# Merging two softmax maps: from VectorE and GpSimd arithmetic to a ScalarE scaling and an accumulating DMA

## The chip, the cores and the metric

The kernel runs on one core of a Trainium2 chip. A core has TensorE (PE in the profile, its weight loads PEld), VectorE (DVE), ScalarE (ACT), GpSimd (POOL), and SyncE (SP), from whose queue this kernel issues its DMAs. The metric is the time of one execution in microseconds on the device, the median of several runs.

## The reference

The program is one layer of a diffusion backbone: 2048 latent tokens and 128 context tokens of width 1024, with a differential attention (4 heads, two softmax maps each) beside a gated short convolution, an output projection and a SwiGLU feed-forward. All is float32. The change concerns the attention, where latent queries attend to 2048 latent and 128 cached keys:

```python
s = jnp.einsum('bqhmd,bkhmd->bhmqk', qblk.astype(jnp.float32), kf) * ATTN_SCALE
p = jax.nn.softmax(s, axis=-1)
a = p[:, :, 0] - lam * p[:, :, 1]          # the two maps of a head, merged
return jnp.einsum('bhqk,bkhe->bqhe', a, vf)
```

Each head's output is then RMS-normalised, which makes it insensitive to a common factor of a row. The kernel uses that: it merges the unnormalised exponentials as e0 + wt * e1, where wt is -lam times the ratio of the two row sums.

## The kernel before

Every float32 matmul is made of products of a high and a low part (`split`, L79: ScalarE casts to the high part, L81, another engine subtracts for the low one, L82). The work goes through these stages: modulation and input projection (to about 384 us), attention with the convolution as filler (384 to about 1316 us), output projection, and the feed-forward.

The attention loops over 4 heads and, within a head, over 8 groups of 256 latent queries and one group of 128 context queries (`work`, L790). For each group `softmaxes` (L485) is called, and after it `values` (L523) for the group before, so that the scores of one group stand in the program ahead of the values of the last.

`softmaxes` goes over the query tiles of 128 of its group, two for a latent group, so there are 64 latent tiles. For each of the two maps of a tile it takes a buffer e of 128 x 2176 float32 and fills it in five chunks of 436 or 432 keys: TensorE makes the scores (L499, into one of three PSUM banks), VectorE scales them into e and takes their maximum (L502). One ScalarE exponential over the 2176 columns, with the row sum, follows (L507). When both maps are there, VectorE works out wt (L510 to L513), and the maps are merged into e[0]: GpSimd scales the last 960 columns of e[1] by wt (L516) and adds them to those of e[0] (L517), and VectorE does the first 1216 columns in one operation (L518).

`values` transposes the merged tiles block by block (17 blocks of 128 keys, two to a PSUM bank, both query tiles, L543), splits them (L546) and multiplies them by the values (L534 to L536). Behind it, the head norm runs with small steps on GpSimd (L90, L91, L573).

There are five buffers for e and, while the convolution lasts, a sixth that every sixth request takes (`e_tile`, L478). e[1] is free after the merge; e[0] after the last transpose of its group.

The convolution is the filler: a generator that yields after some TensorE work (L605 to L667), and `pump` (L778) takes from it at a rate set by `RATE`, after each score chunk and each pair of transposed blocks. Its inputs fu come by 256 KB DMAs from SyncE's queue (L597), five buffers for each part; its tail is a row of GpSimd steps (L657 to L661).

The code is written with a framework that plans the order of each engine's instructions when the program is built, by program order as priority and a simulated timeline, and places the semaphores. Each engine then runs its list in that order.

Of the kernel before, what the change touches and what calls it, by code (L numbers as in the profile page):

```python
# [11 lines left out]
AF = mybir.ActivationFunctionType  # L12
ALU = mybir.AluOpType
# [16 lines left out]
LI = 0.2  # L30

KC = ((0, 436), (436, 436), (872, 436), (1308, 436), (1744, 432))

POOLW = 960
WLV = (2,)
RAWS = 6
RATE = (670, 1500)
# [3 lines left out]
def layer(ctx, tc, x_prompt, x_sample, cache_k, cache_v, cond, w_ada, b_ada, gcol,  # L41
# [3 lines left out]
    V, S, G, T = nc.vector, nc.scalar, nc.gpsimd, nc.tensor  # L45
# [432 lines left out]
    def e_tile():  # L478

        ecount[0] += 1  # L480
        if x_fu is not None and ecount[0] % 6 == 0:
            return pf.tile([P, NALL], F32, tag="e", name="e")
        return pa.tile([P, NALL], F32, tag="e", name="e", bufs=5)

    def softmaxes(qt, nq, km, kcs):  # L485

        nk = sum(n for _, n in kcs)
        sm = pa.tile([P, 2, 2], F32, tag="sm", name="sm", bufs=3)
        r = pa.tile([P, 2, 2], F32, tag="r", name="r", bufs=3)
        out = []  # L490
        for t in range(nq):
            e = []
            for m in range(2):
                et = e_tile()
                mx = pa.tile([P, 5], F32, tag="mx", name="mx", bufs=4)
                for ci, (k0, n) in enumerate(kcs):
                    ps = pss.tile([P, 512], F32, tag="s", name="s")
                    for s in range(2):
                        mm = T.matmul(ps[:, :n], qt[:, s, m, t * P:(t + 1) * P], km[m][:, k0:k0 + n],  # L499
                                      start=(s == 0), stop=(s == 1))  # L500
                        marks.append(mm.ins)
                    V.tensor_scalar(et[:, k0:k0 + n], ps[:, :n], SCALE, None, op0=ALU.mult, op1=ALU.max,  # L502
                                    accum_out=mx[:, ci:ci + 1])
                    pump()
                nm = pa.tile([P, 1], F32, tag="nm", name="nm", bufs=4)
                V.tensor_reduce(nm, mx[:, :len(kcs)], axis=AX.X, op=ALU.max, negate=True)  # L506
                S.activation(et[:, :nk], et[:, :nk], AF.Exp, bias=nm, scale=1.0, accum_out=sm[:, t, m:m + 1])  # L507
                e.append(et)

            V.reciprocal(r[:, t, :], sm[:, t, :])  # L510
            wt = pa.tile([P, 1], F32, tag="wt", name="wt", bufs=3)
            V.tensor_scalar(wt, r[:, t, 1:2], neglam, sm[:, t, 0:1], op0=ALU.mult, op1=ALU.mult)
            V.tensor_scalar(wt, wt, 1e30, -1e30, op0=ALU.min, op1=ALU.max)  # L513
            cut = nk - (POOLW if nk > 128 else 0)
            if cut < nk:
                G.tensor_scalar(e[1][:, cut:nk], e[1][:, cut:nk], wt, 1.0, op0=ALU.mult, op1=ALU.mult)  # L516
                G.tensor_tensor(e[0][:, cut:nk], e[0][:, cut:nk], e[1][:, cut:nk], op=ALU.add)  # L517
            V.scalar_tensor_tensor(e[0][:, :cut], e[1][:, :cut], wt, e[0][:, :cut],  # L518
                                   op0=ALU.mult, op1=ALU.add)
            out.append(e[0])  # L520
        return out, r

# [255 lines left out]
    def pump():  # L778

        nonlocal credit  # L780
        credit += RATE[x_fu is None]
        while credit > 0:
            with tc.issue_after(marks[-1]) if marks else ExitStack():
                c = next(todo)
            if not c:
                credit = 0.0
                break
            credit -= c
# [5 lines left out]
    for n, (h, i) in enumerate(work):  # L794
        if i == 0:
            qt = hb.pop("q") if n == 0 else load_q(h, 0, 256)
            km, kp = hb.pop("k") if n == 0 else load_keys(h)
            vts = load_values(h)
        lat = i < 8
        if i > 0:  # L800
            qt = load_q(h, i, 256 if lat else 128)
        if lat:
            ar = softmaxes(qt, 2, km, KC)
        else:
            ar = softmaxes(qt, 1, [kp[:, 0, :], kp[:, 1, :]], ((0, 128),))
        if pending:
            values(*pending)
        pending = (h, i, ar, vts if lat else vts[17:], 17 if lat else 1)
        ready = max(0, n - 28)
# [347 lines left out]
```

## Time and profile before

| | us |
|---|---|
| median of 3 runs | 3038.56 (3036.72 to 3039.07) |
| the profiled execution | 3041.68 |
| its span, first to last instruction | 3039.9 |
| attention stage (384 to 1316 us) | 932 |
| TensorE busy in that stage | 893.3 |
| VectorE, ScalarE, GpSimd busy there | 738.1, 553.1, 467.0 |
| granted TensorE clock, whole span | 0.987 |

A line of the profile's groups reads: line of the kernel, engine, operation, what is written <- what is read, shape, number; then busy time and mean ns of one; then the idle time of the engine just before, and what ended it. In the views of time a row begins with its start and its length in us. In the digits, each is the busy share of a fortieth of the span in tenths. A wait is put down to the semaphore that came last.

### The profile page before, as it was taken

To read this page: it belongs to the slowest core of one execution; us is meant where nothing else is said; L and a number is where in the kernel's file an instruction comes from. 1 tells how busy PE (TensorE), PEld (TensorE's weight loads), DVE (VectorE), ACT (ScalarE), POOL (GpSimd) and SP (SyncE) were. 2 spreads that over 40 slices of the span, in tenths; PEclk is the share of its full clock that TensorE was granted. 3 is DMA by queue.
4 is the path that set the end of the run, shared out by engine and by line. 5 is a ranking of instruction groups with operands and counts; after the bars stand their busy time and mean duration, and the time that the engine had idled before them with its cause. 6 is when DMAs were issued, how large, how long until landed. Compare 5 with 4: busy or idle time off the path is not lost.

```text
span 3039.9 us, 47168 instructions
## 1 busy us (share of the span) xinstructions
PE 2902.1 (95%) x16925; PEld 2647.5 (87%) x16925; DVE 1961.1 (65%) x3768; ACT 1466.6 (48%) x2707; POOL 1204.6 (40%) x1106
## 2 busy tenths in 40 slices
PE   6999989999999999999999999999999999999998
PEld 4777789998999998988889989999999998788886
DVE  5998477877888888753367765566555554554443
ACT  5333346665556655554455554445444443434332
POOL 5332135455455454522255654555444440111110
PEclk9999999999999999999999999999999999999999
DMA  8886654454354454457554565445633335766663
GB/s 320 286 306 232 197 177 134 133 168 137 119 178 125 120 165 117 127 182 220 173 159 146 151 196 197 152 152 178 231 102 100 104 103 199 243 218 221 217 218 119
DMA packets 353483, 533.64 MB, mean 176 GB/s; under 512 B 33344, under 2 KB 264928, under 8 KB 351456
## 3 DMA queue, kind: packets, MB, share of 16 engines
q1 hardware_dynamic: 353248, 530.62, 54.2%
q8 instruction: 133, 2.18, 0.3%
q14 instruction: 102, 0.84, 0.1%
HBM read 402.18 MB, written 128.34 MB: 175 GB/s over the span
## 4 chain that ended last, share of the span: by engine, by line
PE 63%; DVE 12%; DMA 10%; issue 8%; POOL 4%; ACT 3%; SPq 0%; DVEq 0%; POOLq 0%; ACTq 0%
PE s L499 7%; PE psg L956 6%; PE psg L954 6%; PE psg L955 6%; PE psy L1086 5%; PE psy L1085 5%; PE psy L1084 5%; PE t L543 3%; DMA u2d<-hl 3%; DVE jv L137 2%; DVE wi L82 2%; PE psx L722 2%; PE psx L723 2%; PE psx L721 2%; PE o L536 2%
## 5 line engine op out<-in xcount | busy, mean ns | idle before, releaser
L954 PE MATMUL psg<-u,wi 128*128 128x384 f32 (+1 forms) x1848 | 607.2, 332 | 26.0 <-ACT wi L81 10.3
L956 PE MATMUL psg<-u,wi 128*128 128x384 f32 (+1 forms) x1848 | 597.1, 329 | 10.0 <-DVE wi L82 10.0
L955 PE MATMUL psg<-u,wi 128*128 128x384 f32 (+1 forms) x1848 | 606.5, 328 | 0.0
L502 DVE TENSOR_SCALAR_CACHE_REDUCE e<-s 128x436 f32<-128x436 f32 (+2 forms) x648 | 373.8, 600 | 85.6 <-PE s L499 68.4
L954 PEld LDWEIGHTS psg<-u,wi 128*128 128x128 f32 x1848 | 349.3, 189 | 36.9 <-ACT wi L81 14.2
L956 PEld LDWEIGHTS psg<-u,wi 128*128 128x128 f32 x1848 | 347.8, 189 | 14.0 <-DVE wi L82 13.7
L499 PE MATMUL s<-km,qt 128*128 128x436 f32 (+1 forms) x1280 | 345.7, 374 | 12.3 <-DVE e L502 8.3
L955 PEld LDWEIGHTS psg<-u,wi 128*128 128x128 f32 x1848 | 350.1, 189 | 0.3
L82 DVE TENSOR_TENSOR wi<-st,wi 128x512 fp32r<-128x512 f32 x264 | 245.2, 932 | 157.7 <-ACT wi L81 154.8
L82 DVE TENSOR_TENSOR wo<-rawo,wo 128x1024 fp32r<-128x1024 f32 x132 | 167.0, 1265 | 252.8 <-ACT wo L81 252.8
L507 ACT ACTIVATE e<-e,nm 128x2176 f32<-128x2176 f32 (+1 forms) x136 | 274.0, 2014 | 78.5 <-DVE nm L506 77.8
L81 ACT CAST wi<-st 128x512 fp32r<-128x512 f32 x264 | 163.2, 619 | 279.2 <-PE psg L956 191.1
L1086 PE MATMUL psy<-wo,hhl 128*128 128x512 f32 x748 | 286.1, 391 | 1.8 <-DVE hhl L82 1.8
L1085 PE MATMUL psy<-wo,hhl 128*128 128x512 f32 x748 | 286.7, 391 | 0.9 <-DVE wo L82 0.9
L1084 PE MATMUL psy<-wo,hhl 128*128 128x512 f32 x748 | 286.3, 391 | 0.0
L81 ACT CAST wo<-rawo 128x1024 fp32r<-128x1024 f32 x132 | 139.1, 1054 | 295.4 <-PE psy L1086 285.2
L82 DVE TENSOR_TENSOR wi<-raw,wi 128x512 fp32r<-128x512 f32 x198 | 233.2, 1194 | 35.6 <-ACT wi L81 29.3
L499 PEld LDWEIGHTS s<-km,qt 128*128 128x128 f32 x1280 | 210.6, 192 | 23.3 <-DVE e L502 14.1
L81 ACT CAST ath<-t 128x512 fp32r<-128x512 f32 (+2 forms) x292 | 157.4, 554 | 114.8 <-PE t L543 112.2
L82 DVE TENSOR_TENSOR atl<-t,ath 128x512 fp32r<-128x512 f32 (+2 forms) x292 | 187.2, 649 | 36.4 <-ACT ath L81 35.6
L1057 POOL TENSOR_TENSOR rr<-rr,mhalf 128x1 f32<-128x1 f32 x17 | 13.1, 779 | 452.7 <-DVE rr L1056 452.7
L916 POOL TENSOR_TENSOR st<-raw,st 128x512 f32<-128x512 f32 x66 | 87.2, 1321 | 252.4 <-DVE wi L82 252.4
(261 smaller groups left out, 6991.5 us busy)
## 6 DMA issues: line engine op xcount, KB each, us to landing
raw<-in_w_fi SPq DMA_DIRECT2D x132, 512.0 KB, 4.2
rawo<-in_w_fo SPq DMA_DIRECT2D x132, 512.0 KB, 3.5
fu<-ud SPq DMA_DIRECT2D x256, 256.0 KB, 4.5
raw<-in_w_ada SPq DMA_DIRECT2D x64, 512.0 KB, 5.9
u2d<-hl SPq DMA_DIRECT2D x42, 512.0 KB, 3.9
u<-u2d SPq DMA_DIRECT2D x14, 1536.0 KB, 10.1
hr<-hid SPq DMA_DIRECT2D x110, 192.0 KB, 3.5
hid<-hid SPq DMA_DIRECT2D x88, 192.0 KB, 3.6
```

The costliest lines, as they stand in the source:

```text
L81: S.copy(h, src)
L82: (eng or V).tensor_tensor(l, src, h.bitcast(F32), op=ALU.subtract)
L499: mm = T.matmul(ps[:, :n], qt[:, s, m, t * P:(t + 1) * P], km[m][:, k0:k0 + n], start=(s == 0), stop=(s == 1))
L502: V.tensor_scalar(et[:, k0:k0 + n], ps[:, :n], SCALE, None, op0=ALU.mult, op1=ALU.max, accum_out=mx[:, ci:ci + 1])
L507: S.activation(et[:, :nk], et[:, :nk], AF.Exp, bias=nm, scale=1.0, accum_out=sm[:, t, m:m + 1])
L543: T.transpose(tp[:, j, t * P:(t + 1) * P], a[t][:, (k0 + j) * P:(k0 + j + 1) * P], ident)
L954: T.matmul(ps, h[:, ks], u[:, 0, kt, :n], start=start and kt == 0, stop=False, skip_group_check=not start)
L955: T.matmul(ps, h[:, ks], u[:, 1, kt, :n], start=False, stop=False, skip_group_check=not start)
L956: T.matmul(ps, l[:, ks], u[:, 0, kt, :n], start=False, stop=kt == 3, skip_group_check=not start)
L1084: T.matmul(banks[i][:, b, :], hh, woh_[:, bs], start=(f == 0), stop=False)
L1085: T.matmul(banks[i][:, b, :], hh, wol_[:, bs], start=False, stop=False)
L1086: T.matmul(banks[i][:, b, :], hl, woh_[:, bs], start=False, stop=(f == NF - 1))
```

## The change

For the latent tiles the merge is done in two pieces, columns 0 to 1151 and 1152 to 2175. For each piece ScalarE multiplies e[1] by wt in place (a Copy activation with wt as the scale), and a DMA issued from GpSimd's queue adds the piece to e[0] in place. The context tiles (128 columns) keep VectorE's single operation. The GpSimd arithmetic of L516 and L517 and the constant that set its share are gone.

```diff
-POOLW = 960
...
             V.tensor_scalar(wt, wt, 1e30, -1e30, op0=ALU.min, op1=ALU.max)
-            cut = nk - (POOLW if nk > 128 else 0)
-            if cut < nk:
-                G.tensor_scalar(e[1][:, cut:nk], e[1][:, cut:nk], wt, 1.0, op0=ALU.mult, op1=ALU.mult)
-                G.tensor_tensor(e[0][:, cut:nk], e[0][:, cut:nk], e[1][:, cut:nk], op=ALU.add)
-            V.scalar_tensor_tensor(e[0][:, :cut], e[1][:, :cut], wt, e[0][:, :cut],
-                                   op0=ALU.mult, op1=ALU.add)
+            if nk > 128:
+                for ks in (slice(0, 1152), slice(1152, nk)):
+                    S.activation(e[1][:, ks], e[1][:, ks], AF.Copy, scale=wt)
+                    G.dma_start(e[0][:, ks], e[1][:, ks], accum_op=ALU.add)
+            else:
+                V.scalar_tensor_tensor(e[0][:, :nk], e[1][:, :nk], wt, e[0][:, :nk], op0=ALU.mult, op1=ALU.add)
             out.append(e[0])
```

## The prediction

> **What bounds the kernel now.** I read the page first, for the share of each engine over the span and the chain that ended last.
>
> ```profile
> span 3039.9 us, 47168 instructions
> PE 2902.1 (95%) x16925; PEld 2647.5 (87%) x16925; DVE 1961.1 (65%) x3768; ACT 1466.6 (48%) x2707; POOL 1204.6 (40%) x1106
> ...
> PE   6999989999999999999999999999999999999998
> DVE  5998477877888888753367765566555554554443
> ACT  5333346665556655554455554445444443434332
> POOL 5332135455455454522255654555444440111110
> ...
> PE 63%; DVE 12%; DMA 10%; issue 8%; POOL 4%; ACT 3%; SPq 0%; DVEq 0%; POOLq 0%; ACTq 0%
> ```
>
> TensorE works in nearly every slice, and no other engine comes near it. The change touches only the attention stage, in which VectorE has its highest digits. The first score matmul starts at 384 us and the last merge ends close to 1316 us, so I asked for that stretch, and for TensorE's own groups in it with what ended the idle time before them.
>
> ```profile
> core 0: us, PE busy (x) PEld busy (x) DVE busy (x) ACT busy (x) POOL busy (x), PEclk, DMA share, GB/s
> 384.00:1316.00 932.00, 893.32 (x6449) 857.89 (x6449) 738.10 (x2106) 553.13 (x970) 466.98 (x553) 0.99 0.47 141
> ```
>
> ```profile
> L499 PE MATMUL s<-km,qt 128*128 128x436 f32 (+1 forms) x1280 | 345.7, 374 | 12.3 <-DVE e L502 8.3 <-ACT sto L247 3.7 <-DMA qt<-qd 0.2
> L536 PE MATMUL o<-atl,vv 128*128 128x256 f32 x531 | 167.6, 316 | 2.5 <-DVE atl L82 2.5
> L543 PE MATMUL t<-ident,e 128*128 128x128 f32 x1060 | 164.7, 275 | 8.1 <-DVE nm L506 3.9 <-DVE atl L82 2.8 <-DVE e L518 1.2
> L534 PE MATMUL o<-ath,vv 128*128 128x256 f32 x531 | 152.9, 288 | 2.1 <-ACT ath L81 1.9
> L614 PE MATMUL fc<-fu,bh 128*128 128x256 f32 (+1 forms) x480 | 138.6, 289 | 6.5 <-DMA fu<-ud 6.5
> L615 PE MATMUL fc<-fu,bh 128*128 128x256 f32 (+1 forms) x480 | 138.5, 288 | 3.5 <-DMA fu<-ud 3.4
> ```
>
> In these 932 us TensorE is idle for 932 - 893.3 = 38.7 us. That is the most that any relief of other engines can bring here. Of it, 8.3 + 2.5 + 3.9 + 2.8 + 1.2 = 18.7 us ended on VectorE, 9.9 us on the loads of fu for the convolution, 1.9 us on ScalarE's casts. So the gain that the change can have is small, and the question is what the new, longer way of the merged tile costs.
>
> **The change, part by part.** It touches the merge of the two exponential maps, once for each of 64 query tiles.
>
> ```profile
> L518 DVE SCALAR_TENSOR_TENSOR e<-e,wt 128x1216 f32<-128x1216 f32 x64 | 121.2, 1894 | 0.9
> L516 POOL TENSOR_SCALAR e<-e,wt 128x960 f32<-128x960 f32 x64 | 90.8, 1419 | 137.5 <-DVE wt L513 107.7 <-PE s L499 20.9 <-PE t L543 4.5
> L517 POOL TENSOR_TENSOR e<-e 128x960 f32<-128x960 f32 x63 | 163.5, 2596 | 3.7
> L507 ACT ACTIVATE e<-e,nm 128x2176 f32<-128x2176 f32 x128 | 270.8, 2116 | 74.5 <-DVE nm L506 73.9
> L81 ACT CAST ath<-t 128x512 fp32r<-128x512 f32 x248 | 140.5, 582 | 91.8 <-PE t L543 90.5
> ```
>
> VectorE loses 64 x 1.894 = 121.2 us: from 738.1 to 616.9 of 932, or 79% to 66%. Each of these 1.9 us also stands between two evacuations of scores, so the work behind it comes sooner. Of the 18.7 us that TensorE waits for VectorE I take four fifths back, since a wait behind a busy queue falls faster than the load: -15. The bounds are 0 and all of the idle time, -38.7.
>
> GpSimd loses 90.8 + 163.5 = 254.3 us and gets 128 DMA issues. The trace has no DMA from this engine. The bounds are SyncE's issue of a fu load, quoted below at a median of 421 ns, and the 2.6 us of the addition that goes; I take 1 us, 128 in all. Either way GpSimd is less than half busy. Its queue is in order: an issue waits for ScalarE's scaling, and the convolution's steps (L657 to L661) and the small steps of the head norm (L90, L91, L573) stand behind it. Before, the same steps stood behind L516's wait for wt (107.7 us) and the 4.0 us of the two operations. I count nothing for this: nobody of TensorE waits for these steps soon, and they end sooner once the issue is out. Without that cover it would be 64 times the 1.2 us of a scaling piece, 77 us, spread over the 465 us in which GpSimd is idle now.
>
> ScalarE gets 128 scalings. Between the 512 wide cast (582 ns) and the 2176 wide exponential (2116 ns) lie about 0.92 ns for a column: 1152 columns take 1.2 us, 1024 take 1.1. That is 64 x 2.3 = 147 us: from 553 to 700 of 932, 75%. TensorE's 1.9 us of waiting for its casts grow with the load to 2.4; I take +1 with rounding. If each of the 128 pieces held a cast back by half its length, 0.6 us, and an eighth of that reached TensorE past its two transpose banks, it would be +10, my upper bound.
>
> The merged tile comes later. This is the largest term. Values of a query pair begin with transposes of both tiles; those of the second tile need the merge that has just been made. The first and the last of 32 pairs:
>
> ```profile
> 411.68 1.49 DVE L518 SCALAR_TENSOR_TENSOR e<-e,wt 128x1216 f32<-128x1216 f32 x1
> ...
> 414.25 0.82 PE L543 MATMUL t<-ident,e 128*128 128x128 f32 x6
> ...
> 1315.41 1.49 DVE L518 SCALAR_TENSOR_TENSOR e<-e,wt 128x1216 f32<-128x1216 f32 x1
> ...
> 1316.95 0.65 PEld L543 LDWEIGHTS t<-ident,e 128*128 128x128 f32 x6 [1.11 <-DVE e L518]
> 1316.95 0.88 PE L543 MATMUL t<-ident,e 128*128 128x128 f32 x6 [0.88 <-DVE e L518]
> ```
>
> From the end of L518 to the transposes it is 1.1 us in the first pair and none in the last, where the weight loads wait 1.11 us for it. Over the 32 pairs the median is 2 us. After the change the path from wt to the first columns is a scaling of 1.2 us, an issue and a landing. How long a landing takes is not known for this kind; the nearest rows by size (576 KB and 512 KB) are these:
>
> ```profile
> q1 hardware_dynamic: 130689, 129.83, 46.8%
> ...
> fu<-ud SPq DMA_DIRECT2D x256, 256.0 KB, 4.5
> ...
> wr<-in_w_out SPq DMA_DIRECT2D x4, 512.0 KB, 5.7
> ```
>
> ```profile
> rawo<-in_w_fo SPq DMA_DIRECT2D x132, 512.0 KB, 3.5
> ...
> u<-u2d SPq DMA_DIRECT2D x14, 1536.0 KB, 10.1
> ```
>
> ```profile
> L74 SPq DMA_DIRECT2D fu<-ud x288: 359/421/1956, 396.6 to 1280.8; - x144
> ...
> DMA to landing us min/median/max: 2.6/4.5/9.0
> ```
>
> The lower bound is 3.5 us (512 KB, another stage). The upper is 10.1 us, for 1536 KB: an addition has to read source and destination and write the sum, which makes three times 512 KB of traffic. I take 5.5, near the 5.7 of wr, a load of nearly this size in this very stage. The first columns then come 1.2 + 5.5 = 6.7 us after wt, against 1.9 for L518: 4.8 later. Of this 1.9 us come back, since the first tile's L518 no longer stands ahead of the second tile's score evacuations. The net delay is 2.9 us. In 25 of the 32 pairs the transposes now start less than 2.9 us after L518, and the shortfall sums to 52 us over the pairs. Half of it I expect TensorE to fill with scores of the next pair, once the values before have given back two exponential buffers; the planner puts them there if its own estimate of the DMA is right. That is +26. The bounds are 0 (all filled) and 176, the same sum at a landing of 10.1.
> The second piece lands 1.1 us later. It is late for nobody: its blocks are the last eight of seventeen, which come in the second half of the pair's transposes. It does hold e[1] about 3 us longer than GpSimd's addition did; the waits of L502 for buffers that L517 frees, 8.8 us in 9 cases, are the place where that shows. They are inside the 26.
>
> The transfers share the DMA engines with the fu loads. 64 x 128 x 2176 x 4 bytes are 71.3 MB. The queue moves 129.83 MB in 46.8% of the 16 engines' time, so 71.3 MB at the same cost add 25.7%. TensorE's 9.9 us on fu grow with the share, by 72.5 / 46.8: +5. On this point the Trainium skill (DMA: Bandwidth & Descriptors, section "Issuing engines are not separate DMA queues") says that transfers of all issuing engines run on the same 16 engines and interleave. No row here shows a second issuer; were the transfers separate, this term would be 0 and the sum 5 lower.
>
> **The sum.** -15 + 1 + 26 + 5 = +17 on the profiled execution's own 3041.68 us (span 3039.9 and 1.8 around it): 3058.7. That execution lies 3.1 above the runs' median of 3038.56, so I predict 3055.6, rounded to 3056. A change within 0.2% (6 us) can't be told from none here.
>
> **Rivals.** The landing is hidden (faster). With 3.5 us to land the net delay is 1.2 + 3.5 - 1.9 - 1.9 = 0.9 us; only 14 pairs start sooner than that, for 18 us in all, and the next scores fill these. What stays is -15, +1 and perhaps +2 for fu: 3038.56 - 12 = 3026. For it speaks that VectorE is the engine TensorE waits for most, against it that the rows of this size in this stage are nearer 5.7. It decides below about 4 us of landing. The Trainium skill (DMA: Bandwidth & Descriptors, section "Anatomy of one DMA — SWDGE (gpsimd) path") fits a GpSimd DMA as 2.0 us plus bytes by 436e3; by it 589,824 bytes take an estimated 3.4 us, which is this rival. The row of wr, 5.7 us beside other traffic, speaks for more.
>
> The DMA engines fill (much slower). If an addition costs both its reads, the share rises by 51% to 98%. Landings go to 10.1, of which half of 176 is +88; fu loads go from 4.5 to the 9.0 that is now their longest, and if each of 32 convolution units then waits 1.2 us, +38. With -15 and +1 that gives +112: 3151. It decides from a share of some 90%. Against it: rows of the exponentials are 4 KB and longer, so the added packets should be cheap.
>
> It cancels. Gain and loss are both under 40 us and of one size; a landing of 4.2 makes the net delay 1.6 and the shortfall 28, and -15 + 1 + 14 + 4 is +4: 3043.
>
> The overlap does not happen: in GpSimd's order a convolution step may stand ahead of the issue, and the merge then waits for work that has nothing to do with it. That would add the 1.4 us of a GpSimd operation of the kind of L516 to a path, in all 32 pairs 45 us at most; half of it gives 3078. It lies inside the forecast's range.
>
> **How the numbers follow.** The forecast (slower by more than 6 and less than 70 us, the blocked issue with it) 0.37; DMA full 0.14; cancels 0.17; hidden 0.32. So faster 0.32, same 0.17, slower 0.51. The range must reach into the hidden case, whose -12 can become -18 where ScalarE's and fu's terms vanish: 3021. Upward it takes in the forecast with the ScalarE bound and a landing of 8, and the nearer part of the full case: 3130. The forecast's own range is 3045 to 3100.
>
> **What would show it.** In the changed profile the L518 group of 1216 columns and both GpSimd groups are gone. ScalarE has two new groups of 64 at 1.2 and 1.1 us. VectorE is near 617 us in the stage and ScalarE near 700. The landing of the accumulating DMA stands among the DMA issues: 5.5 by my sum, under 4 for the hidden case, 9 or more for the full one, with the DMA share in the stage near 0.72 or near 0.95. TensorE's transposes wait for that DMA, 20 to 30 us in all, and its waits for fu are near 15 us. Wrong I am if the transposes hardly wait, or if the stage's length changes while TensorE's idle time doesn't.

## The result, and the profile after

The changed kernel takes 3245.27 us (median of 4 runs, 3240.61 to 3252.54) against 3037.64 before: 1.0686 times as long, 95% interval 1.0666 to 1.0705. That is 208 us slower, far above the range that was predicted (3021 to 3130).

The page of the changed kernel, the lines that answer to those shown of before:

```profile
span 3241.8 us, 47415 instructions
...
PE 2969.8 (92%) x16925; PEld 2698.0 (83%) x16925; DVE 1849.3 (57%) x3704; ACT 1602.0 (49%) x2835; POOL 1051.2 (32%) x1106
...
PE   6999888888878888888999999999999999999998
...
DVE  6997455565555555555346676566655554554443
```

TensorE's nines have become eights over the whole attention stage. The stage now runs to 1508 us. Its row among the windows, with TensorE's groups in it:

```profile
384.00:1508.00 1124.00, 959.39 (x6402) 906.47 (x6403) 620.31 (x2037) 683.45 (x1090) 310.64 (x551) 0.92 0.71 178
```

```profile
L497 PE MATMUL s<-km,qt 128*128 128x436 f32 x1278 | 356.0, 386 | 56.3 <-DVE e L500 39.2 <-DMA qt<-qd 12.8 <-ACT sto L245 3.9
L542 PE MATMUL t<-ident,e 128*128 128x128 f32 x1048 | 173.2, 286 | 35.2 <-DMA e<-e 27.3 <-DVE atl L80 5.6 <-ACT on L566 1.2
...
L533 PE MATMUL o<-ath,vv 128*128 128x256 f32 x524 | 157.4, 300 | 36.3 <-ACT ath L79 35.9
...
L613 PE MATMUL fc<-fu,bh 128*128 128x256 f32 (+1 forms) x480 | 146.8, 306 | 28.8 <-DMA fu<-ud 28.8
L614 PE MATMUL fc<-fu,bh 128*128 128x256 f32 (+1 forms) x480 | 146.4, 305 | 7.5 <-DMA fu<-ud 7.2
```

The stage is 1124 us long instead of 932: 192 of the 202 us by which the span grew. Two things in the row make them. TensorE's idle time is 1124 - 959.4 = 164.6 us instead of 38.7, which is 126 more. And its busy time grew by 66 us for the same matmuls, because the granted clock fell from 0.99 to 0.92. The idle time now ends on VectorE's evacuations (39.2), ScalarE's casts (35.9), the loads of fu (36.0) and the merged tile (27.3). The waits of VectorE and ScalarE show how the first two can have one cause (in a row of this view stand who waited for whom, then the us in total, the number of waits and the longest):

```profile
DVE e L500 <- DMA e<-e: 69.0, 17, 7.2
...
PE s L497 <- DVE e L500: 39.2, 15, 6.0
PE o L533 <- ACT ath L79: 35.9, 22, 10.4
...
ACT e L515 <- DVE wt L511: 27.1, 24, 4.3
```

VectorE, at the head of its queue, waits 69 us for a buffer e that a DMA still holds. Behind it stand its other steps; ScalarE waits for wt, and casts can stand behind that. The timeline (start, length) has one case of VectorE's wait:

```profile
896.09 0.59 ACT L79 CAST ath<-t 128x512 fp32r<-128x512 f32 x1 [0.33 <-PE t L542]
898.57 0.61 DVE L500 TENSOR_SCALAR_CACHE_REDUCE e<-s 128x436 f32<-128x436 f32 x1 [5.88 <-DMA e<-e]
...
899.25 1.09 PE L497 MATMUL s<-km,qt 128*128 128x436 f32 x2 [3.20 <-DVE e L500]
...
900.17 0.69 DVE L80 TENSOR_TENSOR atl<-t,ath 128x512 fp32r<-128x512 f32 x1
900.35 0.41 PE L614 MATMUL fb<-fu,bh 128*128 128x256 f32 x1
...
900.57 0.41 PE L615 MATMUL fb<-fu,bl 128*128 128x256 f32 x1
```

VectorE stands for 5.88 us until a DMA has landed. The subtraction for a cast that ended at 896.7 runs only at 900.17, because it stands behind that wait. TensorE is idle for 3.20 us, and then 256-column matmuls start 0.21 us apart. The windows around it give the clock (next to last column group: PEclk, DMA share, GB/s):

```profile
895.90:899.00 3.10, 0.15 (x2) 0.00 (x0) 0.43 (x1) 0.59 (x1) 0.00 (x0) 0.89 0.59 152
899.00:905.00 6.00, 5.75 (x22) 5.63 (x23) 3.76 (x13) 0.92 (x2) 0.40 (x1) 0.50 0.35 112
906.00:912.00 6.00, 6.00 (x45) 5.89 (x44) 3.39 (x11) 4.01 (x7) 2.50 (x3) 1.00 0.89 237
```

After the gap TensorE gets half its clock for about 6 us and does 22 matmuls, where the 6 us from 906 have 45. So a short wait is paid for a second time. Counted over the stage, the trace has 31 stretches at half clock, 174 us in all; the kernel before has 6 of them, 24 us. The Trainium skill (TensorE: Matmul & The Clock Gate, section "What's actually happening") says that the clock falls to half after an idle window of some 3.4 us and comes back after one of activity; the trace agrees on the half and on the step (the stretches are 3.4, 6.8 or 10.2 us long), but shorter gaps do it too: all 18 of TensorE's gaps over 3 us come with half clock, and so do 11 of the 13 between 2 and 3 us.

The merge itself, by groups, and the DMA view of the stage (of a queue its packets, MB and share of the 16 engines; of an issue its count, KB and median us from issue to landing):

```profile
L516 POOL DMA_DIRECT2D e<-e x126 | 115.2, 915 | 214.3 <-ACT e L515 148.4 <-DVE e L500 25.4 <-DVE nm L504 17.9
...
L515 ACT ACTIVATE e<-e,wt 128x1152 f32<-128x1152 f32 x63 | 79.3, 1259 | 27.4 <-DVE wt L511 27.1
...
L515 ACT ACTIVATE e<-e,wt 128x1024 f32<-128x1024 f32 x63 | 71.7, 1137 | 0.0
```

```profile
q1 hardware_dynamic: 129887, 128.29, 38.1%
q0 software_dynamic: 18144, 70.20, 32.9%
...
fu<-ud SPq DMA_DIRECT2D x256, 256.0 KB, 5.4
e<-e POOLq DMA_DIRECT2D x63, 576.0 KB, 6.7
e<-e POOLq DMA_DIRECT2D x63, 512.0 KB, 8.8
```

The scalings (1.26 and 1.14 us), GpSimd's issue (0.92 us), VectorE's 620 and ScalarE's 683 us are close to what was predicted. The landings, 6.7 and 8.8 us, are longer than the 5.5 that was taken.

### The profile page after: what moved, and what is told of

The parts are those of the page before. It is cut to its first block, busy times and chain, and to the rows that moved or that the text cites. A ratio compares the mean times of both kernels' runs of the same rounds, so it can differ in the third digit from the quotient of the medians.

```text
span 3241.8 us, 47415 instructions
## 1 busy us (share of the span) xinstructions
PE 2969.8 (92%) x16925; PEld 2698.0 (83%) x16925; DVE 1849.3 (57%) x3704; ACT 1602.0 (49%) x2835; POOL 1051.2 (32%) x1106
## 5 line engine op out<-in xcount | busy, mean ns | idle before, releaser
L500 DVE TENSOR_SCALAR_CACHE_REDUCE e<-s 128x436 f32<-128x436 f32 (+2 forms) x648 | 373.4, 603 | 260.9 <-PE s L497 152.9
L497 PE MATMUL s<-km,qt 128*128 128x436 f32 (+1 forms) x1280 | 356.6, 386 | 56.3 <-DVE e L500 39.2
L497 PEld LDWEIGHTS s<-km,qt 128*128 128x128 f32 x1280 | 222.1, 200 | 70.2 <-DVE e L500 47.0
L542 PE MATMUL t<-ident,e 128*128 128x128 f32 x1092 | 181.0, 287 | 42.9 <-DMA e<-e 33.7
L533 PE MATMUL o<-ath,vv 128*128 128x256 f32 x548 | 165.0, 301 | 38.1 <-ACT ath L79 37.6
```

The source lines that it names most:

```text
L542: T.transpose(tp[:, j, t * P:(t + 1) * P], a[t][:, (k0 + j) * P:(k0 + j + 1) * P], ident)
```

## The experiments

Four suspects are to be told apart: ScalarE's added load; the traffic on the DMA engines; the transposes, which wait for the merged tile; and the buffers, which the DMA holds until it has landed. In all of them the planner orders the engines anew, except where it is said. Idle is TensorE's idle time in the attention stage (stage length less busy time).

| run | us | ratio, 95% interval | idle us |
|---|---|---|---|
| the kernel before | 3037.64 | | 38.7 |
| the change | 3245.27 | 1.0666 to 1.0705 | 164.6 |
| e1_scale_only | 3104.32 | 1.0197 to 1.0256 | 74.8 |
| e9_scaling_unused | 3043.82 | 1.0006 to 1.0030 | 44.4 |
| e10_traffic_beside | 3109.44 | 1.0208 to 1.0278 | 81.7 |
| e6_copy_no_add | 3119.19 | 1.0245 to 1.0305 | 83.7 |
| e4_into_e0_from_e0 | 3109.89 | 1.0215 to 1.0274 | 80.1 |
| e5_into_e1_from_e1 | 3172.60 | 1.0387 to 1.0503 | 122.2 |
| e8_sixteen_rows | 3119.48 | 1.0240 to 1.0300 | 89.5 |
| e11_sixteen_rows_e0 | 3060.08 | 1.0036 to 1.0098 | 46.2 |
| e2_seven_buffers | 3161.43 | 1.0375 to 1.0442 | 114.0 |
| e14_e0_six_fu | 3077.07 | 1.0094 to 1.0176 | 65.7 |
| e7_second_piece_only | 3062.25 | 1.0052 to 1.0111 | 51.6 |
| e13_second_piece_seven | 3032.69 | 0.9980 to 1.0007 | 41.4 |
| e12_before_seven | 3023.38 | 0.9937 to 0.9964 | 34.4 |
| e15_before_six_fu | 3038.48 | 0.9988 to 1.0023 | 40.6 |

### ScalarE's scaling

The first run keeps the scaling and drops the DMA:

```diff
                 for ks in (slice(0, 1152), slice(1152, nk)):
                     S.activation(e[1][:, ks], e[1][:, ks], AF.Copy, scale=wt)
-                    G.dma_start(e[0][:, ks], e[1][:, ks], accum_op=ALU.add)
+                G.tensor_tensor(e[0][:, 1216:nk], e[0][:, 1216:nk], e[1][:, 1216:nk], op=ALU.add)
+                V.tensor_tensor(e[0][:, :1216], e[0][:, :1216], e[1][:, :1216], op=ALU.add)
```

> ScalarE scales both pieces as in the change, but VectorE (first 1216 columns) and GpSimd (the rest) add them to the first map; no accumulating DMA. Late landing or traffic as the cause: within 25 us of the kernel before (3015 to 3065), since the DMA is gone. ScalarE's scaling as the cause (casts held back behind it): 3100 or more, with TensorE's waits for the casts at 25 us or more.

It took 3104, 69 us more than the kernel before, as the theory of ScalarE's load had it; but TensorE's waits for the casts are 18 us, less than that theory wanted. And the edit brings a wait of its own: VectorE's addition now stands at the head of its queue until ScalarE is done.

```profile
DVE e L517 <- ACT e L515: 57.6, 33, 4.3
```

So the next run adds the same number of ScalarE operations of the same width to the kernel before, on a scrap tile (of bfloat16):

```diff
+            if nk > 128:
+                for n in (1152, 1024):
+                    S.activation(jk[:, :n], jk[:, :n], AF.Copy, scale=wt)
             out.append(e[0])
```

> The kernel before, with two more ScalarE operations for each tile (1152 and 1024 columns, scaled by wt, on a scrap tile that nobody reads): ScalarE's added load and its wait for wt alone. The scaling-only run cost 67 us, but there VectorE's addition also waited for ScalarE. If ScalarE's load is what cost it: 3080 or more. If that wait of VectorE was it: 3035 to 3060.

3043.8: 6 us, for 135 us more of ScalarE's time. Its load costs next to nothing. So the 69 us don't come from the load. VectorE's wait on ScalarE is new in that merge, but whether it or the order that the planner chose anew costs them, no run takes apart.

### Traffic without waits

The first try went wrong. Accumulating DMAs between DRAM buffers were added to the kernel before; nothing tied them to the attention, so the planner put them all ahead of the attention, beside the modulation and the projection. It took 3427.02 us (1.1257 to 1.1322) and says nothing on the change.

> The merge of the kernel before, and beside it, from GpSimd's queue, 128 accumulating DMAs of the change's sizes between DRAM buffers for which nobody waits: the traffic without the waits. If traffic is the cause: 3100 or more, with TensorE's waits for fu and qt near the 49 us of the changed kernel. If the waits for the merged tile and its buffer are the cause: 3040 to 3070, and fu's waits under 20 us.

The second try ties them to GpSimd's addition (zd are two scrap tiles in SBUF):

```diff
-                G.tensor_tensor(e[0][:, cut:nk], e[0][:, cut:nk], e[1][:, cut:nk], op=ALU.add)
+                g = G.tensor_tensor(e[0][:, cut:nk], e[0][:, cut:nk], e[1][:, cut:nk], op=ALU.add)
+                if x_fu is not None:
+                    with tc.issue_after(g.ins):
+                        for z in zd:
+                            G.dma_start(z, z, accum_op=ALU.add)
```

> The kernel before, with the two accumulating DMAs for each tile issued right after GpSimd's addition, on scrap tiles in SBUF that nobody else uses (while the convolution lasts): the traffic and the issues, without the waits. If traffic alone explains much of the loss: 3080 or more, with TensorE's waits for fu at 30 us or more. If the buffer held until the landing explains it: 3040 to 3070.

3109.4: 72 us, with no step of the attention waiting for these DMAs. (Their issues also take 114 us of GpSimd's time, and GpSimd waits 6.5 us for the scrap tiles.) The largest wait of its TensorE, and a line of its DMA view:

```profile
PE fc L621 <- DMA fu<-ud: 39.6, 19, 3.8
```

```profile
fu<-ud SPq DMA_DIRECT2D x256, 256.0 KB, 5.8
```

TensorE's waits for fu are 40 us instead of 10, though a load takes only 1.3 us longer (5.8 against 4.5).

### The held buffer and the waiting transposes

Two runs change which tile the DMA reads and writes, with the same bytes; both leave the second map out of the result. In the one e[1] is free after the scaling; in the other the transposes of e[0] wait for no DMA:

```diff
-                    G.dma_start(e[0][:, ks], e[1][:, ks], accum_op=ALU.add)
+                    G.dma_start(e[0][:, ks], e[0][:, ks], accum_op=ALU.add)    # e4
+                    G.dma_start(e[1][:, ks], e[1][:, ks], accum_op=ALU.add)    # e5
```

> The change with the DMA adding e[0] to itself (leaves the second map out of the result): the same traffic and the transposes wait as before, but e[1] is free after the scaling. If the buffers held by the DMA are the main cause: 3100 or less, and VectorE's waits for DMA landings before L500 (65 us) are near 0. If traffic or the transposes' waits are: 3200 or more.

> The change with the DMA adding e[1] to itself (leaves the second map out of the result): the same traffic, e[1] held until the landing, but the transposes of e[0] wait for no DMA. If the transposes' waits are the main cause: 3100 or less. If the held buffers or the traffic are: 3200 or more, with VectorE's waits for landings before L500 near the 65 us of the changed kernel.

The first edit does more than its expectation says. A DMA that adds e[0] to itself reads no e[1], so it waits neither for wt nor for the scaling. It is issued once the exponential of e[0] is done, in the median 8.9 us before the end of the scaling of its piece, where the change issues it 0.3 us after that end. It has landed, in the median again, 1.3 us before the scaling ends (in the change 8.2 us after it), so the transposes wait for no landing either. The waits of this run:

```profile
POOL e L516 <- ACT e L505: 221.9, 36, 17.8
...
DVE e L500 <- ACT e L515: 59.9, 28, 4.0
...
PE fc L613 <- DMA fu<-ud: 48.2, 19, 8.9
...
PE o L533 <- ACT ath L79: 15.2, 11, 3.1
...
PE s L497 <- DVE e L500: 3.7, 4, 2.0
```

It took 3109.9, so with e[1] free and the transposes not waiting, 135 us of the loss are gone, and what remains is about what the traffic cost beside the kernel before (3109.4). VectorE's L500 waits for no landing any more. It still waits 59.9 us for buffers until ScalarE has scaled them, but never over 4.0 us, and hardly any of that reaches TensorE (3.7 us).

In the second run e[1] is held as in the change, and the transposes wait for nothing of the merge. It took 3172.6, between the two expectations; its VectorE still waits for landings:

```profile
DVE e L500 <- DMA e<-e: 68.7, 21, 7.2
...
PE s L497 <- DVE e L500: 48.8, 19, 9.1
```

So freeing the transposes alone is worth 73 us (3245.3 to 3172.6), and freeing e[1] as well another 63 (to 3109.9). The 73 are more than the 27.3 us that TensorE waits at the transposes in the change. A late transpose also keeps e[0], which comes out of the same six buffers, and gaps are paid for again in the clock; how the 73 us divide is not shown. The order of the engines differs in each of these runs, and its share in the 73 and the 63 is not known.

A buffer more in the change, while the convolution lasts, should relieve both:

```diff
-        if x_fu is not None and ecount[0] % 6 == 0:
-            return pf.tile([P, NALL], F32, tag="e", name="e")
+        if x_fu is not None and ecount[0] % 3 == 0:
+            return pf.tile([P, NALL], F32, tag="e", name="e", bufs=2)
```

> The change with one more buffer for the exponentials while the convolution lasts (every third request goes to a pool of two instead of every sixth to a pool of one). If the buffers held until the landing are the main cause: 3130 or less. If traffic or the transposes' waits are: 3200 or more.

3161.4: 84 us better than the change, less than the 115 that the theory wanted. VectorE's waits for landings did not fall: they are 92.5 us here, and TensorE's for L500 47.0. What fell are TensorE's waits at the transposes (27.3 to 4.8 us) and for the casts (35.9 to 12.4). The buffer exists for the same part of the stage as the sixth only, and the requests that go to the smaller pool, two of six, come round after six requests as before.

### The length of the landing

This run alone has the very order of the changed kernel on every engine. The DMA copies the piece instead of adding it:

```diff
-                    G.dma_start(e[0][:, ks], e[1][:, ks], accum_op=ALU.add)
+                    G.dma_start(e[0][:, ks], e[1][:, ks])
```

> The change with the DMAs copying the piece over the first map instead of adding to it (leaves the first map out); the order of every engine is that of the changed kernel. If what the addition itself costs in the DMA engines makes the landing late: landings fall from 6.7 and 8.8 to about 4 and 5 us, the queue's share in the stage from 33% to about 18%, and the time to 3080 to 3150. If GpSimd's kind of DMA is slow to land whatever it does: landings over 6 us and 3200 or more.

Its DMA view, and waits in it:

```profile
q0 software_dynamic: 18144, 70.20, 18.7%
...
e<-e POOLq DMA_DIRECT2D x63, 576.0 KB, 5.3
e<-e POOLq DMA_DIRECT2D x63, 512.0 KB, 6.5
```

```profile
PE o L533 <- ACT ath L79: 28.0, 19, 3.6
...
DVE e L500 <- DMA e<-e: 23.7, 11, 3.5
...
PE t L542 <- DMA e<-e: 11.7, 9, 2.9
...
PE s L497 <- DVE e L500: 6.2, 7, 1.8
```

3119.2. With nothing changed but the operation, the landings are 1.4 and 2.3 us shorter and 126 us of the loss are gone. As the order is the same, the waits can be set side by side: TensorE's for L500 fall from 39.2 to 6.2 us, for fu from 36 to 12, at the transposes from 27.3 to 11.7, for the casts only from 35.9 to 28.0. So most of the waits for casts don't hang on the length of the landing. The addition takes 32.9% of 1124 us of the DMA engines, the copy 18.7% of 1002: 370 against 187 us, twice as much for the same bytes. With 16 of 128 rows (`e[0][:16, ks], e[1][:16, ks]`), and with these rows of e[0] added to themselves:

> The change with DMAs of 16 of the 128 partitions, one row for each DMA engine (leaves the second map out of the other 112 rows): an eighth of the traffic, with the same issues, waits and dependences. If size and traffic make the landing late: landings of 2 to 4 us and 3030 to 3080. If the fixed way through GpSimd's queue does: landings over 5 us and 3150 or more.

> The change with DMAs of 16 partitions that add e[0] to itself (leaves the second map out): little traffic, e[1] free after the scaling, transposes wait for a landing of some 4 us. Beside the sixteen-row run (3119) it takes away the held buffer; beside the run with e[0] added to itself (3110) it takes away the traffic. If the hold is the larger part of what is left: 3060 or less. If neither matters and ScalarE's scaling does: 3100 or more.

The landing is then still 4.2 us, for 72 KB:

```profile
e<-e POOLq DMA_DIRECT2D x63, 72.0 KB, 4.2
```

The runs took 3119.5 and 3060.1. The second is issued early too (8.8 us before the end of the scaling), so the 59 us between them are the price of the held buffer and of the waiting transposes (21.6 us of TensorE's time in the first) together, and a landing of 4.2 us isn't short enough to hide it. The first run fits neither expectation: it was to be 3080 or less by size, and over 5 us of landing by the way through the queue. An eighth of the bytes isn't an eighth of the engines' time either: 10.6% of 1007 us, or 107 us, against 370. And though its landings are shorter than the copy's, it is no faster (3119.5 and 3119.2), and its VectorE waits longer for them (40.9 us and 23.7): beside the length of the landing, the order of the steps matters.

### How 1 us on a load costs 30

What was open: whether the fu buffers are too few for the longer landing or the DMA engines lack throughput. Six pairs of fu instead of five (`bufs=5` to `bufs=6`), in the run that adds e[0] to itself, and in the kernel before as a control:

> The change with the DMA adding e[0] to itself (leaves the second map out), and six instead of five buffers for each part of fu. If the fu buffers are too few for a landing that takes 1 to 2 us longer: 3070 or less, and TensorE's waits for fu under 20 us. If the DMA engines lack throughput: 3095 or more, and fu's waits still 40 us or more.

> The kernel before with six instead of five buffers for each part of fu: the control. TensorE waits 10 us for fu there. Too few fu buffers: 3020 to 3032. No shortage before: 3033 to 3043.

3077.1 against 3109.9 with five, which lies between the two expectations, and 3038.5 against 3036.2 in the kernel before. So the shortage of buffers is about 33 of the 74 us that the run with five lost; TensorE waits 22 us for fu there (17.8 and 4.6) instead of 51. The rest, some 40 us, is not taken apart further. The two groups in the run with six pairs:

```profile
PE fc L613 <- DMA fu<-ud: 17.8, 8, 6.0
...
PE fc L614 <- DMA fu<-ud: 4.6, 2, 2.9
```

### Half of the change, and a better version

Only the second piece by ScalarE and DMA, VectorE merging the first 1152 columns; then the same with the seventh buffer:

```diff
+                c = 1152
+                S.activation(e[1][:, c:nk], e[1][:, c:nk], AF.Copy, scale=wt)
+                G.dma_start(e[0][:, c:nk], e[1][:, c:nk], accum_op=ALU.add)
+                V.scalar_tensor_tensor(e[0][:, :c], e[1][:, :c], wt, e[0][:, :c], op0=ALU.mult, op1=ALU.add)
```

> Only the second piece (1024 columns) is scaled by ScalarE and added by DMA; VectorE merges the first 1152 in one operation, GpSimd's arithmetic is gone. The first transposes wait for no DMA, and traffic is under half. If the first transposes' wait is the main cause: 3020 to 3070. If the hold of e[1] and the traffic are: 3090 to 3160.

> Only the second piece by ScalarE and DMA, with one more buffer for the exponentials. Without that buffer it was 3062. If the hold was what it lost: 3025 to 3045, the traffic being half. If the traffic was: 3050 to 3065.

3062.3 and 3032.7: with the buffer it can't be told from the kernel before. The 3062.3 was expected if the waiting transposes were the main cause; but this run also shortens the hold (VectorE waits 24.6 us for landings instead of 69.0) and halves the traffic, so it doesn't tell these apart. The control is the kernel before with that buffer:

> The kernel before with one more buffer for the exponentials while the convolution lasts. It is the control for the run of the change with that buffer (3161). If buffers are short in the kernel before as well: 3020 or less. If they only became short with the DMA: 3030 to 3045.

3023.4, 0.9950 of the kernel before (0.9937 to 0.9964), again between the two expectations: the fastest version of all, and without any DMA in the merge. Its stage and its waits of L502 for GpSimd's addition (8.8 us before):

```profile
384.00:1306.00 922.00, 887.56 (x6422) 853.25 (x6421) 730.33 (x2102) 553.08 (x966) 473.95 (x552) 0.99 0.47 141
```

```profile
DVE e L502 <- POOL e L517: 2.2, 2, 1.9
```

## Why the prediction was wrong

- **What bounds the kernel**: right. The gain could be 38.7 us at most, and lay in this stage.
- **VectorE's relief, -15**: it did lose its 121 us (620 busy), but TensorE's waits for it rose from 18.7 to 45 us (39.2 at the scores, 5.6 at the transposes), since VectorE itself now stands before buffers that aren't free.
- **ScalarE, +1**: right for its load, 6 us in the run that tries it alone. But TensorE's waits for its casts were to be 2.4 us and came to 35.9; 28.0 remain in the copy run and 15.2 in the run that adds e[0] to itself, and no run says how many of these belong to the scalings.
- **The merged tile comes later, +26**: this is the step that failed. It priced one wait, that of the transposes, and there TensorE's own wait came out near it (27.3 us; partly luck, as the landing was longer than was taken). But it took the buffers for free: the held e[1] stood "inside the 26" on the strength of 8.8 us of waits in the kernel before, and e[0], kept longer by its late transposes, was not priced. The runs put 135 us on the two (3245 to 3110): 73 with the transposes freed, another 63 with e[1] freed. Buffers were short already, as the 14 us show that the kernel before gains from one more; the longer hold became 69 us of waiting at the head of VectorE's queue.
- **The landing, 5.5 us**: too short, 6.7 and 8.8. The estimate by the Trainium skill (DMA: Bandwidth & Descriptors, section "Anatomy of one DMA — SWDGE (gpsimd) path"), 3.4, was still shorter; even 72 KB took 4.2. The copy run shows that what the addition adds, in landing and in engine time, is worth 126 us.
- **fu beside the traffic, +5**: the share of the DMA engines came out right (0.71 against 0.725) by luck. The transfers were to take 25.7% of 932 us, 240 us, and took 370; the share is what it is because the stage grew. The price was wrong as well: 72 us in the run that has the traffic beside the kernel before, and in the run that adds e[0] to itself a shortage of fu buffers made 33 of its 74 us. Waits didn't grow in proportion to a share.
- **Not in the sum**: TensorE's clock. Its half-rate stretches added 66 us of busy time, about half of the 126 us of idle time that came with them.

The rival of full DMA engines (3151) came nearest, and part of its reason held: it put the additions at 51% of 932 us, 475 us of the engines, so the measured 370 lie between it and the forecast; the landing of the second piece came near its 9 us. But the engines were busy for 0.71 of the stage, not near 0.95, and a load of fu took 5.4 us, not 9.0. The blocked issue was no cause: the issue starts 0.3 us after its scaling in the median, and only once in 128 over 2 us after it. In the hidden rival one reading can't stand: 14 pairs that are each short by at most 0.9 us sum to 12.6 us at most, not 18; its 3026 doesn't rest on it.

The 72 us for the traffic and the 135 make up the 208 nearly, and this is partly luck: they come from two different kernels, and the run that adds e[0] to itself has ScalarE's scalings and VectorE's relief, which the run with traffic alone has not.

## What to carry to other kernels

Before a merge is made slower, count its buffers: how many are live over a period, and what waits at the head of which queue for the next one. A longer landing is then a loss for all that is queued behind that wait, even if the engine that it relieves was the busier one. Gaps on TensorE cost about one and a half times their length here (126 us of idle time came with 66 of lost clock); and where such waits show already, one more buffer is the change to try first. And when a run takes one suspect away, look at what its DMA now waits for: a DMA that no longer reads a tile is issued earlier, and then two suspects are gone.

## What was not expected of the hardware

- An accumulating DMA from SBUF to SBUF took twice the DMA engines' time of a copy of the same bytes (370 against 187 us for 70.2 MB), and landed in 6.7 and 8.8 us instead of 5.3 and 6.5.
- An eighth of the rows did not make the landing an eighth: 4.2 us for 72 KB against 6.7 for 576 KB. Nor was its time on the DMA engines an eighth: 107 us against 370.
- In the run whose accumulating DMAs went to DRAM ahead of the attention, they landed in 31 us, with the DMA engines busy for more than nine tenths:

```profile
zs<-in_w_fi POOLq DMA_DIRECT2D x43, 576.0 KB, 31.0
```
